# Gated linear attention with decays relative to the border of a chunk pair, one score product over 128 rows for both heads, and unscaled states

## The chip, the cores and the metric

The kernel runs on one core of a Trainium2 chip. Its engines work at the same time, each on its own list of instructions in order: TensorE (PE, with its weight loads as PEld), VectorE (DVE), ScalarE (ACT), GpSimd (POOL), and SP, which here issues most transfers. The metric is the device time of one execution in microseconds (us), as the median of several runs. TensorE's clock has two levels, 1.2 and 2.4 GHz; the profile gives the granted clock as a share of the higher one.

## What is computed

One layer of a hybrid trunk over 1024 tokens of width 1024, in float32: a normalised input is projected, three branches run on it (DeltaNet, gated linear attention, S5), are gated and summed, and a gated MLP and an embedding step follow. The change lies in the second branch, with 4 heads of key width 64 and value width 128:

```python
def gla_rule(q, k, v, g_log):
    q, k, v, g_log = map(to_chunks, (q, k, v, g_log))      # chunks of 64 tokens
    b = jnp.cumsum(g_log, axis=3)
    q_e = q * jnp.exp(b)
    k_e = k * jnp.exp(-b)
    attn = jnp.where(incl, jnp.einsum('bnhtd,bnhsd->bnhts', q_e, k_e), 0.0)
    intra = jnp.einsum('bnhts,bnhsv->bnhtv', attn, v)
    k_dec = k * jnp.exp(b[..., -1:, :] - b)
    dS = jnp.einsum('bnhck,bnhcv->bnhkv', k_dec, v)
    g_end = jnp.exp(b[..., -1, :])

    def step(S, inp):
        qe, ds, ge = inp
        o = jnp.einsum('bhck,bhkv->bhcv', qe, S)
        return ge[..., None] * S + ds, o
    ...
    o = intra + jnp.moveaxis(inter, 0, 1)
```

The head outputs are normalised, gated and go on to the merge of the branches.

## The kernel before

The work is laid out with features on the 128 partitions and the 1024 tokens along the free axis, two heads of gated linear attention to a tile (64 partitions each, a "pair"). Tokens go in 8 groups g of 128 (NG = 8), each a pair of chunks of 64.

Phase "1" runs the first norm, narrow (the small projections: rates of DeltaNet, and the log decays of gated linear attention, which are summed within a chunk and written to DRAM as gbd), and the four DeltaNet heads. Phase "2" runs the S5 blocks and gated linear attention in the order of the string ORDER, "P0 U0 U1 C0 A0 U2 C1 B0 U3 C2 A1 C3 B1": U and C are input and core of an S5 block, A is gla_prepare and B is gla_scan of a pair. Then come s5_glu, the output unit of S5, and the remaining gates. The later phases do the merge, the MLP and the output.

gla_prepare (line 702) loads the log decays, forms three exponentials (eb, ek, ed) and multiplies them by the row norm R, projects q and k (proj_in, 48 products of 128x512 each, in the split form hi/lo), and makes qe, q2, ke, kd and k2, where q2 and k2 carry an extra decay for the half of the group that lies across the border of its two chunks. k2 and the two heads' values are transposed on TensorE into kt and vt.

gla_scan (line 765) goes through the tokens in two halves of four groups. For each head and group, line 776 forms the scores from 64 partitions of ke and qe, and line 777 overwrites the quarter across the border from kd and qe. The scores are copied to SBUF (at) and masked, and line 791 multiplies them with the values; line 790 adds the part of the state, from 64 partitions of q2 and state. Line 796 forms the increment of the state (pd) and line 801 the new state. Then come head_norm of each head's outputs and, after both halves, gated_out with the projection of the gate.

In narrow, line 392 multiplies 64 partitions of nar with the constant both, and line 419 takes 48 partitions of the constant w2 and of nar.

Tiles of one tag share the slots of that tag (slot, with the counts given to phase); PSUM has two slots of [128, 1024] (big, tiles pb) and four of one bank (pst, tiles ps, pa, po, pd). A planner fixes the order of the instructions on each engine ahead of time by priorities; fill hands it gates (products of the branch gates, which need nothing from here) to be laid into gaps. In s5_glu, line 1045 loads the four S5 blocks into the slots qe, q2, ke and kd, and line 1054 puts two splits into vt.

Of the kernel before, what the change touches and what calls it, by code (L numbers as in the profile page):

```python
# [20 lines left out]
L = 1024  # L21
# [68 lines left out]
class Trunk:  # L90
# [212 lines left out]
    def constants(self):  # L303
# [36 lines left out]
        nc.gpsimd.memset(self.w2[64:128, :], 0.0)  # L340
        for p in (64, 96):
            self.dma("x", self.w2[p:p + 16, :], self.A["gla_w2"])
        self.both = c.tile([64, 8], F32, name="both")
        nc.gpsimd.tensor_copy(self.both, self.ident[0:64, 0:8])
# [40 lines left out]
    def narrow(self):  # L385
# [5 lines left out]
        for g in range(NG):  # L391
            self.mm(pt[:, g, :], self.nar[0:64, g * 128:(g + 1) * 128], self.both)
# [22 lines left out]
        for pair in range(2):  # L415
            x = self.slot(("kt", "vt")[pair])
            for t in (0, 512):
                pb = self.pst([128, 512])
                self.mm(pb, self.w2[64:112, pair * 128:(pair + 1) * 128], self.nar[64:112, t:t + 512])
                self.act(x[:, t:t + 512], pb, AF.Identity, bias=self.vec("gla_b2", pair, pair + 1))  # L420
# [281 lines left out]
    def gla_prepare(self, pair):  # L702
        nc = self.nc
# [3 lines left out]
        c64 = lambda ap: ap.rearrange("p (c t) -> p c t", t=64)  # L707
        bend = c64(gb)[:, :, 63:64].to_broadcast([128, 16, 64])
        eb, ek, ed = (self.slot(n) for n in ("qe", "ke", "kd"))
        self.sub(c64(ed), bend, c64(gb))  # L710
        self.act(ed, ed, AF.Exp, scale=1.0 / 16)
        self.act(eb, gb, AF.Exp, scale=1.0 / 16)
        self.act(ek, gb, AF.Exp, scale=-1.0 / 16)
        ee = self.sm([128, 16], "gla_ee")
        nc.vector.tensor_copy(ee, c64(eb)[:, :, 63])
        eev = ee.rearrange("p (g a) -> p g a", a=2)
        ge = self.sm([128, NG], "gla_ge")
        self.mul(ge, eev[:, :, 0], eev[:, :, 1])
        pair_v = lambda ap: ap.rearrange("p (g a t) -> p g a t", a=2, t=64)
        for e in (eb, ek, ed):  # L720
            self.mul(e, e, self.R)

        ps = self.proj_in(base)
        qe = eb
        self.stt(qe, ps, 0.125, eb, ALU.mult, ALU.mult)
        q2 = self.slot("q2")
        self.copy(pair_v(q2)[:, :, 0, :], pair_v(qe)[:, :, 0, :])
        self.mul(pair_v(q2)[:, :, 1, :], pair_v(qe)[:, :, 1, :],
                 eev[:, :, 0:1].to_broadcast([128, NG, 64]))
# [4 lines left out]
        kd = ed  # L734
        self.mul(kd, ps, ed)
        k2 = self.slot("t")
        self.copy(pair_v(k2)[:, :, 1, :], pair_v(kd)[:, :, 1, :])
        self.mul(pair_v(k2)[:, :, 0, :], pair_v(kd)[:, :, 0, :],
                 eev[:, :, 1:2].to_broadcast([128, NG, 64]))
        kt = self.slot("kt", (128, NG, 128))  # L740
        for half in range(2):
            pt = self.pst([128, 4, 128])
            for i in range(4):
                g = 4 * half + i
                self.tr(pt[:, i, :], k2[:, g * 128:(g + 1) * 128])
            self.copy(kt[:, 4 * half:4 * half + 4, :], pt)

        vt = []
        for hd in range(2):
# [3 lines left out]
            vtk = self.slot("vt", (128, NG, 128))  # L753
            for half in range(2):
# [4 lines left out]
                self.copy(vtk[:, 4 * half:4 * half + 4, :], pt)  # L759
            vt.append(vtk)  # L760
        self.fill("gla")
        return qe, q2, ke, kd, kt, vt, ge

    @ranked
    def gla_scan(self, pair, prepared):
        nc = self.nc
        qe, q2, ke, kd, kt, vt, ge = prepared
        state = None
        for half in range(2):
            ats, pos = [], []  # L770
            for hd in range(2):
                p0 = slice(64 * hd, 64 * hd + 64)
                pa = self.pst([128, 4, 128], "pa")
                for i in range(4):
                    t0 = (4 * half + i) * 128
                    self.mm(pa[:, i, :], ke[p0, t0:t0 + 128], qe[p0, t0:t0 + 128])
                    self.mm(pa[0:64, i, 64:128], kd[p0, t0:t0 + 64], qe[p0, t0 + 64:t0 + 128])
                at = self.t2k([128, 4, 128], "gla_at")
                self.copy(at, pa)
                nc.vector.copy_predicated(at, self.imask.unsqueeze(1).to_broadcast([128, 4, 128]),  # L780
                                          self.zero.unsqueeze(1).to_broadcast([128, 4, 128]))
                ats.append(at)
            for hd in range(2):
                pos.append(self.pst([128, 4, 128], "po"))
            for i in range(4):
                g = 4 * half + i
                for hd in range(2):
                    p0 = slice(64 * hd, 64 * hd + 64)
                    if state is not None:
                        self.mm(pos[hd][:, i, :], q2[p0, g * 128:(g + 1) * 128], state[p0, :], stop=False)  # L790
                    self.mm(pos[hd][:, i, :], ats[hd][:, i, :], vt[hd][:, g, :], start=state is None)
                if g < NG - 1:
                    pd = self.pst([128, 128], "pd")
                    for hd in range(2):
                        p0 = slice(64 * hd, 64 * hd + 64)
                        self.mm(pd[p0, :], kt[:, g, p0], vt[hd][:, g, :])
                    new = self.t5h([128, 128], "gstate")
                    if state is None:
                        nc.vector.tensor_copy(new, pd)
                    else:  # L800
                        self.stt(new, state, ge[:, g:g + 1], pd, ALU.mult, ALU.add)
                    state = new
            self.fill(f"gscan{half}")
            for hd in range(2):
                po = pos[hd]
# [784 lines left out]
```

## Time and profile before

| | us |
|---|---|
| median of 3 runs | 1924.6 (1923.9 to 1927.0) |
| profiled execution | 1922.1 |
| its span, first to last instruction | 1920.4 |
| TensorE busy | 1878.0 |
| VectorE busy | 1308.1 |
| ScalarE busy | 716.3 |
| first scan (gla_scan of pair 0) | 620.5 to 662.6 |
| second scan (pair 1) | 810.05 to 846.86 |

A busy time is the time in which at least one instruction of the engine runs. Matmuls overlap, so the distance between the starts of two of them tells what one costs, not its duration. In the rows further below "x8" is a count of instructions, a shape such as 64*128 behind a matmul is the part of TensorE's array that it uses (rows*columns), a float32 product is two instructions, and PEclk is the granted clock.

### The profile page before, as it was taken

How to read it: one execution, taken by the hardware profiler on the slowest of the kernel's cores; microseconds unless marked ns; L12 is line 12 of the kernel's file. 1: busy time of each engine (PE TensorE's matmuls, PEld its weight loads, DVE VectorE, ACT ScalarE, POOL GpSimd, SP SyncE). 2: the span in 40 equal slices, each digit the busy share in tenths (PEclk: the TensorE clock that was granted, in tenths of full speed). 3: DMA queues.
4: the chain of work that ended last, by engine and by line, in shares of the span. 5: the costliest groups of instructions: out<-in, count | busy, mean ns of one | idle time of the engine just before them, and what ended most of it. 6: DMA issues, size and time to landing. Idle time of an engine off the chain costs nothing.

```text
span 1920.4 us, 25126 instructions
## 1 busy us (share of the span) xinstructions
PE 1878.0 (98%) x9213; PEld 1535.8 (80%) x9213; DVE 1308.1 (68%) x2748; ACT 716.3 (37%) x1122; POOL 42.8 (2%) x64
## 2 busy tenths in 40 slices
PE   7999999999999999999899999999999999999998
PEld 5788887878888788777688878888888888878887
DVE  6898777765876576555467577787878774475446
ACT  5632332323423232323222444443434454363335
POOL 4000000000100000000000000000000000000000
PEclk9899999999999899989999999999999999999999
DMA  5123131221333133324754522222222257364332
GB/s 179 65 75 98 56 97 42 72 96 59 117 83 102 61 107 94 93 88 180 252 170 135 169 90 77 88 77 88 80 90 82 94 164 250 111 202 149 99 112 83
DMA packets 114844, 212.55 MB, mean 111 GB/s; under 512 B 25153, under 2 KB 38689, under 8 KB 114721
## 3 DMA queue, kind: packets, MB, share of 16 engines
q1 hardware_dynamic: 106080, 183.68, 29.9%
q10 hardware_dynamic: 8640, 27.27, 4.3%
q8 instruction: 72, 1.18, 0.2%
q14 instruction: 52, 0.42, 0.1%
HBM read 159.22 MB, written 51.68 MB: 110 GB/s over the span
## 4 chain that ended last, share of the span: by engine, by line
PE 71%; DVE 4%; ACT 1%; DMA 1%; issue 1%; POOLq 0%; DVEq 0%; ACTq 0%; POOL 0%
PE pb L166 35%; PE ps L166 31%; PE po L166 2%; PE pa L166 1%; DVE H L141 1%; PE ps L170 1%; DMA r<-yd 1%; PE pd L166 1%; DVE s_pa L141 0%; DVE s_pb L141 0%; PE pu L166 0%; DVE lo L141 0%; DMA raw<-cd 0%; DVE wl L141 0%; ACT hi L160 0%
## 5 line engine op out<-in xcount | busy, mean ns | idle before, releaser
L166 PE MATMUL pb<-hi,wh 128*128 128x512 f32 x1260 | 407.5, 400 | 17.1 <-DVE wh L141 8.1
L160 ACT ACTIVATE wh<-wr 128x512 fp32r<-128x512 f32 (+1 forms) x335 | 204.2, 614 | 573.0 <-PE pb L166 348.5
L166 PE MATMUL pb<-lo,wh 128*128 128x512 f32 x1260 | 403.9, 398 | 3.4 <-DVE lo L153 3.0
L166 PE MATMUL pb<-hi,wl 128*128 128x512 f32 x1244 | 399.3, 397 | 0.0
L141 DVE TENSOR_TENSOR wl<-wr,wh 128x512 fp32r<-128x512 f32 (+1 forms) x333 | 221.5, 669 | 196.9 <-ACT wh L160 187.6
L166 PEld LDWEIGHTS pb<-hi,wh 128*128 128x128 f32 x1260 | 236.7, 191 | 68.9 <-DVE wh L141 8.1
L166 PEld LDWEIGHTS pb<-lo,wh 128*128 128x128 f32 x1260 | 238.2, 190 | 55.3 <-DVE lo L153 4.7
L166 PEld LDWEIGHTS pb<-hi,wl 128*128 128x128 f32 x1244 | 234.1, 190 | 48.7 <-issue 2.6
L166 PE MATMUL ps<-hi,wh 128*128 128x512 f32 x442 | 172.8, 391 | 0.0
L166 PE MATMUL ps<-hi,wl 128*128 128x512 f32 x442 | 172.5, 390 | 0.0
L166 PE MATMUL ps<-lo,wh 128*128 128x512 f32 x442 | 172.4, 390 | 0.0
L166 PEld LDWEIGHTS ps<-hi,wh 128*128 128x128 f32 x442 | 83.3, 188 | 17.4
L166 PEld LDWEIGHTS ps<-hi,wl 128*128 128x128 f32 x442 | 83.2, 188 | 17.3
L166 PEld LDWEIGHTS ps<-lo,wh 128*128 128x128 f32 x442 | 83.2, 188 | 17.2
L160 ACT ACTIVATE fh<-wr 128x512 fp32r<-128x512 f32 x65 | 40.9, 632 | 114.7 <-PE ps L166 72.4
L153 DVE SCALAR_TENSOR_TENSOR c<-z,vecs,c 128x1023 f32<-128x1023 f32 (+1 forms) x44 | 56.5, 1284 | 6.9 <-ACT c L160 6.1
L166 PE MATMUL ps<-ph,wh 128*128 128x512 f32 (+1 forms) x128 | 49.2, 384 | 0.0
L166 PE MATMUL ps<-pl,wh 128*128 128x512 f32 (+1 forms) x128 | 48.5, 379 | 0.1
L166 PE MATMUL ps<-ph,wl 128*128 128x512 f32 (+1 forms) x128 | 48.3, 377 | 0.0
L141 DVE TENSOR_TENSOR z<-s,pb 128x512 f32<-128x512 f32 x44 | 30.2, 687 | 23.1 <-PE pb L166 23.1
L141 DVE TENSOR_TENSOR fl<-wr,fh 128x512 fp32r<-128x512 f32 x65 | 44.6, 688 | 1.8 <-ACT fh L160 1.8
L141 DVE TENSOR_TENSOR sgm<-pb,R 128x1024 f32<-128x1024 f32 x24 | 29.1, 1221 | 24.1 <-PE pb L166 24.0
(469 smaller groups left out, 3173.4 us busy)
## 6 DMA issues: line engine op xcount, KB each, us to landing
wr<-in_w_up SPq DMA_DIRECT2D x88, 256.0 KB, 2.8
wr<-in_w_down SPq DMA_DIRECT2D x80, 256.0 KB, 2.7
wr<-in_w_in SPq DMA_DIRECT2D x66, 256.0 KB, 3.2
wr<-in_w_gate SPq DMA_DIRECT2D x48, 256.0 KB, 2.9
gd<-sgm SPq DMA_DIRECT2D x24, 512.0 KB, 2.9
sgl<-gd ACTq DMA_DIRECT2D x24, 512.0 KB, 4.2
cd<-c SPq DMA_DIRECT2D x22, 512.0 KB, 2.6
wr<-in_w_ple_gate SPq DMA_DIRECT2D x32, 256.0 KB, 2.9
```

The costliest lines, as they stand in the source:

```text
L141: self.nc.vector.tensor_tensor(out=out, in0=a, in1=b, op=op)
L153: self.nc.vector.scalar_tensor_tensor(out=out, in0=a, scalar=s, in1=b, op0=op0, op1=op1)
L160: self.nc.scalar.activation(out, a, func, scale=scale, **kw)
L166: self.nc.tensor.matmul(out, lhsT=lhsT, rhs=rhs, start=start, stop=stop, **kw)
L170: self.nc.tensor.transpose(out, in_, self.ident[0:n, 0:n])
```

## The change

The log decays are taken relative to the border between the two chunks of a group: within the first chunk they are subtracted from the chunk's end, the second chunk counts from its start. With decays written so, one product over a whole group of 128 tokens gives the scores, and kd, q2 and k2 fall away. The queries of the two heads are written into one tile qm of [128, 2, 1024], for each head zero on the other head's 64 partitions, so that one product with all 128 partitions of ke gives the scores of both heads (256 columns). The states are kept unscaled (total); for the outputs a copy of the state, scaled by dec on ScalarE, is multiplied with all 128 partitions of qm. The increments of a half share one PSUM tile and come first. The values of both heads share one tile vt; s5_glu uses the slots qm, ke, kd and vt. In narrow the two small products take all 128 partitions, with zeros in the constants.

```diff
--- before.py
+++ after.py
@@ -337,11 +337,12 @@
         self.hbglu = c.tile([128, 4], F32, name="hbglu")
         nc.vector.tensor_scalar_mul(self.hbglu, self.vec("s5_b_glu"), 0.5)
         self.w2 = c.tile([128, 256], F32, name="w2")
-        nc.gpsimd.memset(self.w2[64:128, :], 0.0)
+        nc.gpsimd.memset(self.w2, 0.0)
         for p in (64, 96):
             self.dma("x", self.w2[p:p + 16, :], self.A["gla_w2"])
-        self.both = c.tile([64, 8], F32, name="both")
-        nc.gpsimd.tensor_copy(self.both, self.ident[0:64, 0:8])
+        self.both = c.tile([128, 8], F32, name="both")
+        nc.gpsimd.memset(self.both, 0.0)
+        nc.gpsimd.tensor_copy(self.both[0:32, :], self.ident[0:32, 0:8])
         nc.gpsimd.tensor_copy(self.both[32:64, :], self.ident[0:32, 0:8])
 
 
@@ -389,7 +390,7 @@
         self.mul(self.nar, ps, self.R)
         pt = self.pst([128, NG, 8])
         for g in range(NG):
-            self.mm(pt[:, g, :], self.nar[0:64, g * 128:(g + 1) * 128], self.both)
+            self.mm(pt[:, g, :], self.nar[:, g * 128:(g + 1) * 128], self.both)
         c = self.cpool
         sh = [128, HEADS, NG]
         b = self.sm(sh, "n_b")
@@ -416,7 +417,7 @@
             x = self.slot(("kt", "vt")[pair])
             for t in (0, 512):
                 pb = self.pst([128, 512])
-                self.mm(pb, self.w2[64:112, pair * 128:(pair + 1) * 128], self.nar[64:112, t:t + 512])
+                self.mm(pb, self.w2[:, pair * 128:(pair + 1) * 128], self.nar[:, t:t + 512])
                 self.act(x[:, t:t + 512], pb, AF.Identity, bias=self.vec("gla_b2", pair, pair + 1))
             ab = self.slot(("kt", "vt")[pair])
             self.stt(ab, x, -1.0, x, ALU.mult, ALU.max)
@@ -700,114 +701,116 @@
 
     @ranked
     def gla_prepare(self, pair):
+
         nc = self.nc
         base = 16 + 6 * pair
         gb = self.slot("t")
         self.dma("ld", gb, self.gbd[pair])
-        c64 = lambda ap: ap.rearrange("p (c t) -> p c t", t=64)
-        bend = c64(gb)[:, :, 63:64].to_broadcast([128, 16, 64])
-        eb, ek, ed = (self.slot(n) for n in ("qe", "ke", "kd"))
-        self.sub(c64(ed), bend, c64(gb))
-        self.act(ed, ed, AF.Exp, scale=1.0 / 16)
-        self.act(eb, gb, AF.Exp, scale=1.0 / 16)
-        self.act(ek, gb, AF.Exp, scale=-1.0 / 16)
-        ee = self.sm([128, 16], "gla_ee")
-        nc.vector.tensor_copy(ee, c64(eb)[:, :, 63])
-        eev = ee.rearrange("p (g a) -> p g a", a=2)
-        ge = self.sm([128, NG], "gla_ge")
-        self.mul(ge, eev[:, :, 0], eev[:, :, 1])
         pair_v = lambda ap: ap.rearrange("p (g a t) -> p g a t", a=2, t=64)
-        for e in (eb, ek, ed):
+        gv = pair_v(gb)
+        ee = self.sm([128, NG, 2], "gla_ee")
+        self.act(ee, gv[:, :, :, 63], AF.Exp, scale=1.0 / 16)
+        end = self.sm([128, NG, 1], "gla_end")
+        self.copy(end, gv[:, :, 0, 63:64])
+        self.sub(gv[:, :, 0, :], end.to_broadcast([128, NG, 64]), gv[:, :, 0, :])
+
+        dec = self.sm([128, NG - 1], "gla_dec")
+        self.mul(dec, ee[:, 0:NG - 1, 1], ee[:, 1:NG, 0])
+        eq, ek = self.slot("kd"), self.slot("ke")
+        for e, s in ((eq, 1.0 / 16), (ek, -1.0 / 16)):
+            self.act(pair_v(e)[:, :, 0, :], gv[:, :, 0, :], AF.Exp, scale=-s)
+            self.act(pair_v(e)[:, :, 1, :], gv[:, :, 1, :], AF.Exp, scale=s)
             self.mul(e, e, self.R)
 
+        qm = self.slot("qm", (128, 2, L))
+        for hd in range(2):
+            nc.gpsimd.memset(qm[64 - 64 * hd:128 - 64 * hd, hd, :], 0.0)
         ps = self.proj_in(base)
-        qe = eb
-        self.stt(qe, ps, 0.125, eb, ALU.mult, ALU.mult)
-        q2 = self.slot("q2")
-        self.copy(pair_v(q2)[:, :, 0, :], pair_v(qe)[:, :, 0, :])
-        self.mul(pair_v(q2)[:, :, 1, :], pair_v(qe)[:, :, 1, :],
-                 eev[:, :, 0:1].to_broadcast([128, NG, 64]))
+        for hd in range(2):
+            p0 = slice(64 * hd, 64 * hd + 64)
+            self.stt(qm[p0, hd, :], ps[p0, :], 0.125, eq[p0, :], ALU.mult, ALU.mult)
 
         ps = self.proj_in(base + 1)
         ke = ek
         self.mul(ke, ps, ek)
-        kd = ed
-        self.mul(kd, ps, ed)
-        k2 = self.slot("t")
-        self.copy(pair_v(k2)[:, :, 1, :], pair_v(kd)[:, :, 1, :])
-        self.mul(pair_v(k2)[:, :, 0, :], pair_v(kd)[:, :, 0, :],
-                 eev[:, :, 1:2].to_broadcast([128, NG, 64]))
         kt = self.slot("kt", (128, NG, 128))
         for half in range(2):
             pt = self.pst([128, 4, 128])
             for i in range(4):
                 g = 4 * half + i
-                self.tr(pt[:, i, :], k2[:, g * 128:(g + 1) * 128])
+                self.tr(pt[:, i, :], ke[:, g * 128:(g + 1) * 128])
             self.copy(kt[:, 4 * half:4 * half + 4, :], pt)
 
-        vt = []
+        vt = self.slot("vt", (128, NG, 2, 128))
         for hd in range(2):
             ps = self.proj_in(base + 2 + hd)
             vc = self.slot("t")
             self.mul(vc, ps, self.R)
-            vtk = self.slot("vt", (128, NG, 128))
             for half in range(2):
                 pt = self.pst([128, 4, 128])
                 for i in range(4):
                     g = 4 * half + i
                     self.tr(pt[:, i, :], vc[:, g * 128:(g + 1) * 128])
-                self.copy(vtk[:, 4 * half:4 * half + 4, :], pt)
-            vt.append(vtk)
+                self.copy(vt[:, 4 * half:4 * half + 4, hd, :], pt)
         self.fill("gla")
-        return qe, q2, ke, kd, kt, vt, ge
+        return qm, ke, kt, vt, dec
 
     @ranked
     def gla_scan(self, pair, prepared):
         nc = self.nc
-        qe, q2, ke, kd, kt, vt, ge = prepared
-        state = None
+        qm, ke, kt, vt, dec = prepared
+        sh = [128, 2, 2, 128]
+        flat = lambda t: t.rearrange("p i h t -> p (i h) t")
+        total = None
         for half in range(2):
-            ats, pos = [], []
-            for hd in range(2):
-                p0 = slice(64 * hd, 64 * hd + 64)
-                pa = self.pst([128, 4, 128], "pa")
-                for i in range(4):
-                    t0 = (4 * half + i) * 128
-                    self.mm(pa[:, i, :], ke[p0, t0:t0 + 128], qe[p0, t0:t0 + 128])
-                    self.mm(pa[0:64, i, 64:128], kd[p0, t0:t0 + 64], qe[p0, t0 + 64:t0 + 128])
-                at = self.t2k([128, 4, 128], "gla_at")
+            ats, pos, states = [], [], []
+            pd = self.pst([128, 4, 128], "pd")
+            for i in range(4):
+                g = 4 * half + i
+                if g < NG - 1:
+                    for hd in range(2):
+                        p0 = slice(64 * hd, 64 * hd + 64)
+                        self.mm(pd[p0, i, :], kt[:, g, p0], vt[:, g, hd, :])
+            for j in range(2):
+                pa = self.pst(sh, "pa")
+                for i in range(2):
+                    t0 = (4 * half + 2 * j + i) * 128
+                    self.mm(pa[:, i], ke[:, t0:t0 + 128], qm[:, :, t0:t0 + 128])
+                at = self.t2k(sh, "gla_at")
                 self.copy(at, pa)
-                nc.vector.copy_predicated(at, self.imask.unsqueeze(1).to_broadcast([128, 4, 128]),
+                nc.vector.copy_predicated(flat(at), self.imask.unsqueeze(1).to_broadcast([128, 4, 128]),
                                           self.zero.unsqueeze(1).to_broadcast([128, 4, 128]))
                 ats.append(at)
-            for hd in range(2):
-                pos.append(self.pst([128, 4, 128], "po"))
+            for i in range(4):
+                g = 4 * half + i
+                if g:
+                    states.append(self.tmp([128, 128], "gstate", "gstate", 4))
+                    self.copy(states[-1], total, scale=dec[:, g - 1:g])
+                if g < NG - 1:
+                    new = self.t5h([128, 128], "gtotal")
+                    if g == 0:
+                        nc.vector.tensor_copy(new, pd[:, i])
+                    else:
+                        self.stt(new, total, dec[:, g - 1:g], pd[:, i], ALU.mult, ALU.add)
+                    total = new
+            for j in range(2):
+                pos.append(self.pst(sh, "po"))
             for i in range(4):
                 g = 4 * half + i
                 for hd in range(2):
-                    p0 = slice(64 * hd, 64 * hd + 64)
-                    if state is not None:
-                        self.mm(pos[hd][:, i, :], q2[p0, g * 128:(g + 1) * 128], state[p0, :], stop=False)
-                    self.mm(pos[hd][:, i, :], ats[hd][:, i, :], vt[hd][:, g, :], start=state is None)
-                if g < NG - 1:
-                    pd = self.pst([128, 128], "pd")
-                    for hd in range(2):
-                        p0 = slice(64 * hd, 64 * hd + 64)
-                        self.mm(pd[p0, :], kt[:, g, p0], vt[hd][:, g, :])
-                    new = self.t5h([128, 128], "gstate")
-                    if state is None:
-                        nc.vector.tensor_copy(new, pd)
-                    else:
-                        self.stt(new, state, ge[:, g:g + 1], pd, ALU.mult, ALU.add)
-                    state = new
+                    po = pos[i // 2][:, i % 2, hd, :]
+                    if g:
+                        self.mm(po, qm[:, hd, g * 128:(g + 1) * 128], states[i - (half == 0)], stop=False)
+                    self.mm(po, ats[i // 2][:, i % 2, hd, :], vt[:, g, hd, :], start=g == 0)
             self.fill(f"gscan{half}")
-            for hd in range(2):
-                po = pos[hd]
+            for j in range(2):
+                po = flat(pos[j])
                 r = self.head_norm(po, 4)
-                self.mul(vt[hd][:, 4 * half:4 * half + 4, :], po, r.unsqueeze(2).to_broadcast([128, 4, 128]))
+                g0 = 4 * half + 2 * j
+                self.mul(flat(vt[:, g0:g0 + 2]), po, r.unsqueeze(2).to_broadcast([128, 4, 128]))
         for hd in range(2):
             hh = 2 * pair + hd
-            self.gated_out(self.proj_in(16 + 6 * pair + 4 + hd), vt[hd], self.hgla, "t", "t", self.yd[1][hh])
+            self.gated_out(self.proj_in(16 + 6 * pair + 4 + hd), vt[:, :, hd, :], self.hgla, "t", "t", self.yd[1][hh])
 
 
     def cmul(self, outr, outi, ar, ai, br, bi, tmp):
@@ -1040,18 +1043,19 @@
     @ranked
     def s5_glu(self):
         nc = self.nc
-        ys, raws = [], []
-        for q in range(4):
-            raw = self.slot(("qe", "q2", "ke", "kd")[q])
+        ys = []
+        qm = self.slot("qm", (128, 2, L))
+        raws = [qm[:, 0], qm[:, 1], self.slot("ke"), self.slot("kd")]
+        for q, raw in enumerate(raws):
             self.dma("ld", raw, self.y5d[q])
-            raws.append(raw)
             hi = self.slot(("up", "ub", "F", "H")[q], dt=F32R)
             lo = self.slot(("up", "ub", "M", "E")[q], dt=F32R)
             self.split(raw, hi, lo)
             ys.append((hi, lo))
         self.pt = []
+        his = self.slot("vt", (128, 2, L), F32R)
         for k in range(2):
-            hi, lo = self.slot("vt", dt=F32R), self.slot(("kt", "G")[k], dt=F32R)
+            hi, lo = his[:, k], self.slot(("kt", "G")[k], dt=F32R)
             raw = self.gpool.tile([128, L], F32, tag="sg", name="sgp", bufs=2)
             self.dma("ld", raw, self.A["pT"][k * 128:(k + 1) * 128, :])
             self.split(raw, hi, lo)
@@ -1480,8 +1484,8 @@
                         dn[h] = self.dn_prepare(h)
                     if h:
                         self.dn_scan(h - 1, dn.pop(h - 1))
-            slots = {t: 2 for t in ("up", "ub", "t", "vt")}
-            slots.update({t: 1 for t in ("F", "E", "G", "M", "H", "qe", "q2", "ke", "kd", "kt")})
+            slots = {t: 2 for t in ("up", "ub", "t")}
+            slots.update({t: 1 for t in ("F", "E", "G", "M", "H", "qm", "ke", "kd", "kt", "vt")})
             with self.phase("2", slots, {"t2k": 4, "t1k": 2, "t5h": 4}):
                 u, gl = {}, {}
                 U = lambda q: u.__setitem__(q, self.s5_in(q))
```

## Rows read from the trace of the kernel before

**Rows 1.** The page, part 1: busy us (share of the span) xinstructions.

```profile
PE 1878.0 (98%) x9213; PEld 1535.8 (80%) x9213; DVE 1308.1 (68%) x2748; ACT 716.3 (37%) x1122; POOL 42.8 (2%) x64
```

**Rows 2.** Windows, instructions on pb alone: window, length, PE busy (xcount), PEclk, DMA.

```profile
620.50:662.60 42.10, 13.19 (x34) 0.80 0.19 50
810.05:846.86 36.81, 9.60 (x22) 0.81 0.25 76
```

**Rows 3.** Windows in the scans: length, PE, PEld, DVE, ACT, POOL busy (xcount), PEclk, DMA.

```profile
624.00:630.50 6.50, 6.50 (x22) 4.90 (x22) 1.46 (x2) 0.60 (x1) 0.00 (x0) 0.50 0.27 44
...
641.00:651.70 10.70, 10.70 (x34) 7.90 (x35) 4.49 (x19) 1.12 (x2) 0.00 (x0) 0.53 0.40 138
```

**Rows 4.** Chain of waits: start us, us, what, ahead of the first scan.

```profile
496.67 20.90 PE pb L166 x92
...
617.07 3.57 PE ps L166 x32
```

**Rows 5.** Timeline of PE, scores: start us, us, engine, line, operation, array, shape, count.

```profile
621.24 0.49 PE L166 MATMUL pa<-qe,ke 64*128 64x128 f32 x2
621.65 0.33 PE L166 MATMUL pa<-qe,kd 64*64 64x64 f32 x2
621.90 0.49 PE L166 MATMUL pa<-qe,ke 64*128 64x128 f32 x2
...
625.06 0.79 PE L166 MATMUL pa<-qe,ke 64*128 64x128 f32 x2
625.78 0.47 PE L166 MATMUL pa<-qe,kd 64*64 64x64 f32 x2
```

**Rows 6.** Timeline of PE, increments and outputs of the first scan.

```profile
630.87 0.66 PE L166 MATMUL pd<-vt,kt 128*64 128x128 f32 x8
631.46 0.50 PE L166 MATMUL pb<-hi,wl 128*128 128x512 f32 x1
631.89 0.49 PE L166 MATMUL po<-gstate,q 64*128 64x128 f32 x2
632.30 0.49 PE L166 MATMUL po<-vt,gla_at 128*128 128x128 f32 x2
632.72 0.48 PE L166 MATMUL po<-gstate,q 64*128 64x128 f32 x2
```

**Rows 7.** Timeline of PE, the spread of the first norm.

```profile
46.22 1.03 PE L166 MATMUL ps<-rms_d,ones 128*128 128x256 f32 x4
46.89 0.58 PE L166 MATMUL ps<-hi,k 128*128 128x512 f32 x1
```

**Rows 8.** Windows ahead of the first scan.

```profile
486.00:620.50 134.50, 134.50 (x718) 112.97 (x716) 106.94 (x388) 50.05 (x95) 13.08 (x22) 1.00 0.34 106
```

**Rows 9.** One window of the same kind and the timeline of PE, narrow.

```profile
54.00:64.00 10.00, 10.00 (x17) 4.60 (x16) 7.15 (x9) 6.15 (x8) 0.00 (x0) 0.50 0.00 0
...
57.44 3.78 PE L166 MATMUL ps<-w,w 48*128 48x512 f32 x4
```

**Rows 10.** Tiles qe and ud: operation, xcount: ns min/median/max, first and last start, shape.

```profile
L141 DVE TENSOR_TENSOR qe<-qe,R x2: 1211/1215/1219, 517.6 to 692.3; 128x1024 f32<-128x1024 f32 x2
...
L160 ACT ACTIVATE ud<-pu,cd x28: 348/367/369, 206.6 to 484.0; 128x128 f32<-128x128 f32 x28
```

**Rows 11.** Timeline of SP, its queue in the second scan.

```profile
833.67 0.34 SPq L113 DMA_DIRECT2D qe<-y5d  x1
...
834.71 0.32 SPq L113 DMA_DIRECT2D M<-s5y  x1
...
858.46 0.33 SPq L113 DMA_DIRECT2D kd<-y5d  x1
```

**Rows 12.** Timeline of DVE behind the second scan.

```profile
848.79 1.28 DVE L153 SCALAR_TENSOR_TENSOR M<-up,vecs,M 128x1024 f32<-128x1024 f32 x1
...
863.75 1.22 DVE L141 TENSOR_TENSOR E<-kd,H 128x1024 fp32r<-128x1024 f32 x1
```

**Rows 13.** Timeline of PE, start of s5_glu.

```profile
866.75 1.20 PE L166 MATMUL pb<-up,wh 128*128 128x512 f32 x4 [0.47 <-DVE t L141]
```

## The prediction

> **What bounds the kernel now.** I read the page's busy times first: TensorE is busy for 1878.0 of 1920.4 us, VectorE for 68% [rows 1]. So the question about any edit is how much TensorE time it takes away, and whether what feeds TensorE keeps pace afterwards. Next I read the stages by windows. The two scans of gated linear attention (gla_scan, one for each pair of heads) run at 620.5 to 662.6 us and at 810.05 to 846.86 us [rows 2]. TensorE is busy all the time there, but not at its full clock: in the two long slow stretches of the first scan the granted clock is 0.50 and 0.53, so nearly throughout at the lower level, 1.2 GHz [rows 3], and over either scan it is 0.80 [rows 2]. Then I read TensorE in order of time and along the chain of waits, because a busy time can't tell a fast matmul from a slow one: the distance from one start to the next can.
>
> At the full clock an instruction of a projection (128x512) takes 20.90 / 92 = 0.227 us, and one of the full-shape float32 products of the S5 stage, just ahead of the first scan, 3.57 / 32 = 0.112 us; such a product is two instructions, 0.223 us [rows 4]. The score products of the scan are dearer although they are smaller: at the full clock a call with 64 rows takes 0.41 us and the 64x64 call behind it 0.25 us, at the low level the former takes 0.72 us [rows 5]. The output products show that it isn't the 64 rows alone: a 64-row call (state) and a 128-row call (values) alternate there, and either takes 0.41 us [rows 6]. A full call beside calls of another tile shape costs nearly twice what it costs among its like.
>
> **What the change takes away in the scans.** First the scans as they are. In the first window 34 instructions of projections and gates (tile pb) lie between the scan's own, in the second 22 [rows 2]; at 0.227 us these are 7.7 and 5.0 us, and four transposes in the first are 0.4 us. The scans proper thus cost 42.1 - 8.1 = 34.0 us and 36.8 - 5.0 = 31.8 us, together 65.8 us, low clock included.
>
> After the change, for each pair of heads:
> - Scores: eight calls of 128 rows and 256 columns in place of 32 calls of half the rows. The nearest row is the spread of the norm, four 256-column float32 instructions in 0.67 us, 0.17 us each [rows 7]; twice the 128-column instruction is 0.22 us. I take the dearer, since it holds over a longer stretch: 16 x 0.22 = 3.5 us.
> - Outputs: 16 calls with the values and 14 with the states, all 128x128 now: 30 x 0.223 = 6.7 us. If they kept today's 0.41 us: 12.3 us.
> - State increments (pd): 28 instructions of 64 columns as before, now in two blocks. Eight took 0.59 us [rows 6], so 2.1 us; four changes of shape at 0.19 us (0.41 less 0.22) are 0.8 us.
>
> That is 13.1 us for a pair, 26.2 us for both, so 65.8 - 26.2 = 39.6 us less, if the clock stays full. I expect that: the S5 products, full calls too, run at 1.00 to the end of their stretch [rows 8], and the clock fell only after some microseconds of the half-row calls (the rows at 621 us are still at full price, those at 625 us are not [rows 5]).
>
> Here a rule speaks against the change. The rows say that a 64-row call costs 0.41 us, more than a full one. The Trainium skill, TensorEngine Tiling (Array Packing), section Performance Considerations, recommends two-fold row tiling for a contraction of at most 64, two calls side by side in the array; padding with zeros gives that up. By the rule the old half-row calls would cost half of a full one, the scans some 10 us a pair, and the change would add about 5 us in all. The trace disagrees: one head's calls follow one another on the same rows, shapes alternate, and nothing runs side by side. What the old calls cost is measured, so the rule gets no chance here.
>
> **The small products of narrow.** They take 64 and 48 rows now and 128 afterwards. From 54 to 64 us the granted clock is 0.50 with TensorE busy throughout; four 48-row instructions take 3.8 us [rows 9]. At the full clock these 10 us of work are 5.0 us. So between 0 (the clock falls anyway) and 5.0 us; VectorE, busy for 7.15 of the 10 us [rows 9], follows, so I count 3.5 us.
>
> **What moves on the other engines.** For each pair gla_prepare loses on VectorE the product kd, a multiplication by R (1.215 us each [rows 10]), two half-size products and half a subtraction, and gains a second 64-partition product of 1.215 us: some 3 us less. ScalarE has less to do as well. POOL gets two memsets. All this lies beside projections: in 486 to 620.5 us TensorE is busy for 134.50 of 134.50 us [rows 8]. I cost it at nothing; without that cover a memset that waits for its tile could cost 2 us. That the two value tiles of a pair become one slot costs nothing either: the second pair's scan comes 147 us after the first's [rows 2], so the slot is long free. The larger memsets of w2 and both lie in the first microseconds, and narrow reads them after 50 us. In the scan ScalarE gets 14 scaled copies of the state; the like in DeltaNet takes 0.367 us [rows 10]. They stand between a state and its output products, 5.1 us in all, but the next state doesn't wait for them, and increments, scores and projections can run meanwhile: between 0 and 5.1 us, I take 0, as today's scans leave TensorE no idle time [rows 2].
>
> **Where it can be given back.** Behind the second scan stands the S5 output unit (s5_glu), which needs the last S5 block by way of DRAM. Its load M<-s5y is issued on SP's queue at 834.71 us, behind the load of qe, which had waited until the scan had read its last scores (833.67) [rows 11]. From 848.79 us VectorE works on it, and its last split starts at 863.75 and takes 1.22 us: 16.2 us [rows 12]. TensorE begins the unit at 866.75 us [rows 13], so today the projections behind the scan (from 846.86 us) cover the chain with 1.8 us to spare. In the new kernel the first two loads go into qm, which is read until the last output product. If M<-s5y stays behind them, it is issued only at the scan's end; an estimate of 3 us for it to land (for kd's load it is under 5.3 us, from its issue at 858.46 [rows 11] to the split at 863.75) makes the chain 19.2 us from there against 19.9 us of cover, and two splits that can be done ahead today come on top. So 0 to 10 us; I take 2 us, nearer to the low end, as the chain's own work is unchanged.
>
> **Sum against the profiled run.** 39.6 + 3.5 - 2 = 41.1 us. The profiled execution took 1922.1 us (span 1920.4), 2.5 us under the median of the runs, 1924.6. On the median's scale 1924.6 - 41.1 = 1883.5 us; since shorter scans leave VectorE's chains less cover in places that I can't name, I allow 1.5 us more: 1885 us.
>
> **Rivals.**
> 1. The clock falls all the same, so the change does only half of what it can. The scans' 26.2 us and the 12.7 us of projections among them then run for perhaps half of the time at about 1.7 times their price (0.72 against 0.41): some 13 us lost, and narrow's 3.5 us: 1901 us. For it: no row of before shows a stretch of the new kind, with half of qm zeros and increments of half the columns. Against it: the S5 stretch [rows 8]. Chance 0.12.
> 2. The tail takes it back: behind the second scan the chain is uncovered by 10 to 20 us, 1894 to 1904 us. For it: only 1.8 us to spare, and VectorE works in a fixed order. Against it: its work is the same, and M<-s5y may be placed ahead of the loads into qm. Chance 0.16.
> 3. Slower: the increments of a half now share one PSUM tile that is held until the last of them is added, beside two tiles of scores and two of outputs, five for four slots. The second half's tiles then wait until the first half's norm has read its outputs; if VectorE has long work queued ahead of that norm, TensorE stands still. It turns slower from 10.3 us of uncovered waiting in each of the four halves (41.1 / 4); with 14 us each, 1940 us. Against it: today's second halves wait for the same norm, and projections fill that time [rows 2]. Chance 0.04.
>
> **How the numbers follow.** Forecast 0.65 (its own range 1877 to 1894), clock 0.12, tail 0.16, slower 0.04, little change for reasons not named 0.03. The range takes in the forecast, the clock and most of the tail: 1877 to 1902. Its low end is both gains whole (39.6 + 5.0 us) with the cheaper price of the scores (1.6 us), 1878 us, and 1 us for the spread of the runs. About 0.2% is what a measurement of this kernel can tell from no change: faster by more 0.93, within it 0.03, slower 0.04.
>
> **What would show it.** Right: in the trace of after output calls stand 0.22 us apart, the granted clock is 1.00 in both scans and from 54 to 64 us, and the scans cost about 13 us each without what lies between. Wrong: the low clock in the scans (rival 1); TensorE idle behind the second scan, ended by VectorE's splits (rival 2); TensorE idle ahead of a second half's scores or outputs (rival 3).

## The result

| | before | after |
|---|---|---|
| median, us (four runs; three of after) | 1924.5 | 1893.1 |
| ratio, with its 95% interval | | 0.9830 (0.9809 to 0.9852) |
| profiled execution, us | 1922.1 | 1889.1 |
| its span, us | 1920.4 | 1887.3 |

A fourth run of after took 3076.4 us at a granted clock of 0.56 and is left out here; the other three took 1889.1 to 1894.7 us, and with it the median is 1893.9 us. So the change brings 31.4 us by the medians (the profiled executions stand 33.0 us apart). Forecast was 1885 us: the time lies in the range, 8.1 us above its likeliest value.

### The profile of after

The page of after, its busy times [rows 1 for before] and its granted clock in 40 slices (9 is 0.9 or more); the last line is the clock of before:

```profile
PE 1844.1 (98%) x9117; PEld 1510.4 (80%) x9117; DVE 1303.5 (69%) x2740; ACT 718.7 (38%) x1138; POOL 49.6 (3%) x69
...
PEclk9999999999999999999999999999999999999999
```

```profile
PEclk9899999999999899989999999999999999999999
```

TensorE is busy 33.9 us less, and no slice of after falls below 0.9, where three of before do. The windows of the two scans (window, length, PE busy and count, granted clock, DMA) answer to [rows 2]:

```profile
617.17:632.20 15.03, 15.03 (x118) 1.00 0.25 66
786.14:800.20 14.06, 14.06 (x113) 1.00 0.28 86
```

The scans take 15.0 and 14.1 us in place of 42.1 and 36.8, though with 11 and 8 projection instructions between their own instead of 34 and 22. The timeline of TensorE in the first scan answers to [rows 5, 6]:

```profile
617.17 1.09 PE L166 MATMUL pd<-vt,kt 128*64 128x128 f32 x16
618.19 1.99 PE L166 MATMUL pa<-qm,ke 128*128 128x256 f32 x8
619.84 0.81 PE L166 MATMUL pb<-hi,wl 128*128 128x512 f32 x2
...
621.40 0.39 PE L166 MATMUL po<-gstate,qm 128*128 128x128 f32 x2
621.62 0.39 PE L166 MATMUL po<-vt,gla_at 128*128 128x128 f32 x2
621.85 0.39 PE L166 MATMUL po<-gstate,qm 128*128 128x128 f32 x2
```

An output call follows the one before it by 0.22 us, where it was 0.41; a score instruction takes (619.84 - 618.19) / 8 = 0.206 us, an increment 1.02 / 16 = 0.064 us.

So far the forecast holds. What it lacks comes later. S5's output unit starts at 824.54 us, 42.2 us ahead of [rows 13]:

```profile
824.54 1.09 PE L166 MATMUL pb<-up,wh 128*128 128x512 f32 x4
```

The tile Xh then shows when its products begin and end in the MLP's up stage: the view gives count, duration of one in ns (min/median/max), first and last start. First of before, then of after:

```profile
L166 PE MATMUL ps<-Xh,wh x90: 388/390/632, 1140.8 to 1563.7; 128*128 128x512 f32 x90
```

```profile
L166 PE MATMUL ps<-Xh,wh x90: 392/397/496, 1099.2 to 1531.0; 128*128 128x512 f32 x90
```

After is 41.6 us ahead at the first of them and 32.7 us at the last: 8.9 us are lost in a stage in which the change has not touched a line. A window in the middle of it, of before and of after:

```profile
1200.00:1400.00 200.00, 200.00 (x884) 1.00 0.25 85
```

```profile
1200.00:1400.00 200.00, 200.00 (x864) 1.00 0.25 84
```

TensorE is busy all the time and at its full clock in both, and gets through 20 instructions fewer: 0.2315 us each in place of 0.2262.

### The profile page after: what moved, and what is told of

It is laid out like the page before. It is cut to its first block, busy times and chain, and to the rows that moved or that the text cites. A ratio compares the mean times of both kernels' runs of the same rounds, so it can differ in the third digit from the quotient of the medians.

```text
span 1887.3 us, 24948 instructions
## 1 busy us (share of the span) xinstructions
PE 1844.1 (98%) x9117; PEld 1510.4 (80%) x9117; DVE 1303.5 (69%) x2740; ACT 718.7 (38%) x1138; POOL 49.6 (3%) x69
## 4 chain that ended last, share of the span: by engine, by line
PE 71%; DVE 3%; DMA 1%; ACT 1%; issue 1%; POOLq 0%; DVEq 0%; ACTq 0%; POOL 0%
PE pb L166 37%; PE ps L166 31%; PE po L166 1%; PE ps L170 1%; DMA raw<-cd 1%; DMA r<-yd 1%; DVE H L141 0%; PE pd L166 0%; PE pa L166 0%; DVE lo L141 0%; PE pu L166 0%; ACT hi L160 0%; DVE s_pa L141 0%; DVE s_pb L141 0%; DVE wl L141 0%
```

## Experiments: the loss in the MLP

What the two kernels differ in there is where the tiles lie in SBUF. The change adds two kinds of small tiles, gla_end and gla_dec, and drops gla_ge; each is held in two slots of 32 bytes per partition, so the pool of small tiles grew by 64 bytes. All that the compiler puts behind it, Xh, Xl, the split MLP weights fh, fl and the tiles of every phase among it, moved by 64 bytes: Xh's pool from byte 113856 of each partition to 113920. What lies ahead stayed: hi and lo from 9408, wr, wh and wl from 74944. Theory A is the place; theory B is that this execution happened to be slow.

**The changed kernel again**, as the yardstick (no edit).

> The changed kernel once more, as the yardstick for the three others on the same chip. Theory A (the matmuls of the first MLP products run 2% slower because every tile behind the small tiles has moved by 64 bytes per partition in SBUF) and theory B (that execution happened to be slow there) both expect a median near 1892 us against 1924. They differ in the window from 1200 to 1400 us: A expects 864 matmuls there again (0.2315 us from start to start), B 880 or more.

Measured: 1888.9 us, ratio 0.9819 (0.9804 to 0.9833), 865 instructions in the window. The loss is there again, so it is not the chance of one execution.

**The old addresses.**

```diff
-        end = self.sm([128, NG, 1], "gla_end")
+        end = self.sm([128, NG, 1], "gla_end", bufs=1)
...
-        dec = self.sm([128, NG - 1], "gla_dec")
+        dec = self.sm([128, NG - 1], "gla_dec", bufs=1)
```

> The changed kernel with one slot in place of two for the small tiles gla_end and gla_dec, so that the small tiles take 64 bytes per partition less and all later tiles lie at the addresses of the kernel before; the order of the instructions stays as it is. Theory A (place): 882 to 885 matmuls from 1200 to 1400 us, and about 9 us less than the changed kernel, 1880 to 1886 us. Theory B (not the place): 864 as in the changed kernel, and the same time within 2 us.

Measured: 1876.4 us, ratio 0.9754 (0.9740 to 0.9769), 12.5 us less than the changed kernel, more than the 9 us expected. Window and tile:

```profile
1200.00:1400.00 200.00, 200.00 (x884) 1.00 0.25 82
```

```profile
L166 PE MATMUL ps<-Xh,wh x90: 389/389/499, 1100.0 to 1521.4; 128*128 128x512 f32 x90
```

The stage starts when it did in after (1100.0 against 1099.2 us) and ends 9.6 us sooner. Against e3_after, whose profiled execution took 11.0 us longer, the stage gives 10.4 us of that (421.4 us in place of 431.8 from the first of these products to the last). The duration of a product is 389 ns nearly throughout, where it scatters from 392 to 397 and beyond in after. This version beats both kernels.

**The kernel before, moved by 64 bytes.**

```diff
+        self.sm([128, NG], "gla_x")
```

> The kernel before with one small tile more that nothing uses, so that all later tiles move by the same 64 bytes per partition as in the changed kernel. Theory A (place): about 864 matmuls from 1200 to 1400 us in place of 884, and about 9 us more than before, 1931 to 1935 us. Theory B: the same as before within 2 us.

Measured: 1934.1 us, ratio 1.0053 (1.0037 to 1.0070): a tile that nothing reads makes the old kernel 10.5 us slower. In the profiled execution 7.4 us are lost in this stage (430.3 us in place of 422.9), and its window is that of after:

```profile
1200.00:1400.00 200.00, 200.00 (x864) 1.00 0.25 84
```

Theory A stands, in both directions. What about the place is it that counts? Four more runs change unused tiles: in three of them only the size of the one ahead of the small tiles (PAD) in the changed kernel; the fourth, e9_all_shift64, takes the version with the old addresses and adds a new one ahead of everything.

```diff
-PAD = 32
+PAD = 96
```

> The changed kernel with an unused tile 64 bytes larger, so that all tiles behind it lie 128 bytes further than in the kernel before (64 further than in the changed kernel). If the price of a matmul hangs on the place in steps of 128 bytes: 882 to 885 matmuls from 1200 to 1400 us, and 1876 to 1879 us. If the best place is a single address, or if more bytes are worse: 864 or fewer, and 1888 us or more.

```diff
         self.mpool.tile([128, PAD // 4], F32, name="pad", bufs=1)
+        self.cpool.tile([128, 16], F32, name="pad_all")
```

> The version with the old addresses, and an unused tile of 64 bytes ahead of everything, so that the split weights (wh, wl) move by the same 64 bytes as Xh, Xl and the rest, which then lie at the same addresses as in the changed kernel. If it is the relation of the two operands' addresses that counts: 882 to 885 matmuls from 1200 to 1400 us, and 1876 to 1879 us. If it is the address of Xh and Xl by itself: 864, and 1888 us or more.

PAD = 224 and PAD = 480:

> The changed kernel with an unused tile that is larger, so that Xh, Xl and all tiles behind the small ones lie 256 bytes further than in the kernel before, while the weights stay; in the kernel before the two lie 38912 bytes apart, 19 x 2048. Since 64 and 128 bytes more were both slow: if the distance counts in steps of 256, 884 matmuls from 1200 to 1400 us and 1876 to 1879 us; in steps of 512 or more, 865 to 870 and 1888 us or more.

> The same with 512 bytes more than in the kernel before. If the distance counts in steps of 256 or 512: 884 matmuls from 1200 to 1400 us and 1876 to 1879 us. In steps of 1024 or more: 865 to 870 and 1888 us or more.

Measured, all together (moved: bytes per partition against the kernel before; instructions from 1200 to 1400 us):

| kernel | Xh, Xl, fh, fl moved | hi, lo, wr, wh, wl moved | instructions | median, us | ratio to before |
|---|---|---|---|---|---|
| before | 0 | 0 | 884 | 1922.4 to 1924.1 | 1 |
| e2_before_shift64 | 64 | 0 | 864 | 1934.1 | 1.0053 |
| e3_after | 64 | 0 | 865 | 1888.9 | 0.9819 |
| e8_after_shift128 | 128 | 0 | 869 | 1890.1 | 0.9835 |
| e10_shift256 | 256 | 0 | 885 | 1877.1 | 0.9756 |
| e10_shift512 | 512 | 0 | 884 | 1878.1 | 0.9760 |
| e1_after_old_addr | 0 | 0 | 884 | 1876.4 | 0.9754 |
| e9_all_shift64 | 64 | 64 | 884 | 1878.3 | 0.9772 |

So it is not the address of Xh or fh by itself: in e9_all_shift64 both lie where they lie in after, and the price is the good one. It is how far they have moved against what lies ahead of the small tiles, and of the moves tried, 0, 256 and 512 bytes are good, 64 and 128 are not. My expectation named the two operands of one product as the pair whose distance counts, and that is too narrow. The product of Xh and fh has both operands among the moved tiles, at the same addresses in after and in e9_all_shift64, and yet its duration differs; the tile view of after, then of e9_all_shift64:

```profile
L166 PE MATMUL pb<-Xh,fh x88: 388/392/397, 1112.0 to 1533.8; 128*128 128x512 f32 x88
```

```profile
L167 PE MATMUL pb<-Xh,fh x88: 389/389/389, 1109.5 to 1522.4; 128*128 128x512 f32 x88
```

Whether it is slowed by the products ahead of it in the stream, or by other engines that read wr at the same time, no run here tells. The mechanism stays open; the size is measured, and so are the distances at which it appears. The Trainium skill, SBUF — State Buffer, section Who interferes with whom, lets accesses hold one another up on the port pair that VectorE and GpSimd share and nowhere else; by that rule no distance between tiles could make a matmul wait for another access. Whether such waits are behind the 864 instructions against 884, no run here tells.

## Experiments: the scans

**Narrow alone**: the kernel before with the full-row constants, which get their zeros as in the change.

```diff
...
-            self.mm(pt[:, g, :], self.nar[0:64, g * 128:(g + 1) * 128], self.both)
+            self.mm(pt[:, g, :], self.nar[:, g * 128:(g + 1) * 128], self.both)
...
-                self.mm(pb, self.w2[64:112, pair * 128:(pair + 1) * 128], self.nar[64:112, t:t + 512])
+                self.mm(pb, self.w2[:, pair * 128:(pair + 1) * 128], self.nar[:, t:t + 512])
```

> The kernel before with the narrow part of the change alone (the two small products on all 128 partitions). If rows of 128 keep the clock up: granted clock 1.00 from 54 to 64 us, the first scan 3 to 4 us earlier with its low clock as before, and 3 to 5 us less in all, 1920 to 1922 us. If the clock there falls for another reason: 0.5 as before and no gain.

Measured: 1918.4 us, ratio 0.9971 (0.9960 to 0.9982), 5.2 us less. Windows of this kernel in narrow [rows 9] and in the scores of its first scan:

```profile
54.00:57.00 3.00, 3.00 (x10) 1.00 0.00 0
57.00:60.00 3.00, 3.00 (x12) 1.00 0.00 0
...
622.00:627.00 5.00, 5.00 (x19) 0.50 0.34 59
```

The clock is full in narrow, and falls in the scan as before: what narrow does is not what lowers it in the scan. In before the clock stands at 0.50 from 54 us [rows 9], behind these products of 64 and 48 rows:

```profile
51.43 1.39 PE L166 MATMUL ps<-both,w 64*128 64x8 f32 x11
...
53.10 2.40 PE L166 MATMUL ps<-w,w 48*128 48x512 f32 x3
```

Both kinds were widened together, so which of them lowers it there this run does not tell.

**Scores from 64 rows again, all of one shape.**

```diff
-                    self.mm(pa[:, i], ke[:, t0:t0 + 128], qm[:, :, t0:t0 + 128])
+                    self.mm(pa[:, i], ke[p0, t0:t0 + 128], qm[p0, hd, t0:t0 + 128])
```

(within a loop over heads in place of pairs of groups; the mask and the outputs follow)

> The changed kernel with its scores formed for each head from 64 partitions again (16 calls of 64 rows and 128 columns for each pair in place of 8 of 128 rows and 256 columns), all of one shape in a row. If 64 rows alone cost 0.41 us a call: 0.41 us from start to start, 16 x 0.41 - 3.5 = 3.1 us more for each pair, and if the clock falls in them too, 6 us or more in all, 1895 us or later. If only a change of shape costs: 0.22 us a call, the same price as the calls they replace, and within 2 us of the changed kernel.

Timeline of TensorE, first scan:

```profile
620.00 1.71 PE L166 MATMUL pa<-qm,ke 64*128 64x128 f32 x16
621.64 0.73 PE L166 MATMUL pb<-hi,wl 128*128 128x512 f32 x2
```

Sixteen instructions in 621.64 - 620.00 = 1.64 us, 0.103 each: a 64-row call costs 0.21 us, and two of them, one for each head, cost what the padded call of both heads costs, 2 x 0.206 us. The granted clock is 1.00 in every window of 5 us of the first scan. So 64 rows among their like are neither dear here nor do they lower the clock. The median is 1891.8 us, 2.9 above the yardstick, where I expected at most 2; the score calls explain none of that. Of the 2.4 us between the profiled executions, 0.6 lie ahead of the first scan, 1.0 between the starts of the two scans and 0.8 from there to S5's output unit; in the first scan four output instructions take 0.83 us from 623.17 us, where four took 0.44 in e3_after. Why they come later was not followed.

**State products from 64 rows, in turn with those of 128.**

```diff
-                        self.mm(po, qm[:, hd, g * 128:(g + 1) * 128], states[i - (half == 0)], stop=False)
+                        self.mm(po, qm[p0, hd, g * 128:(g + 1) * 128], states[i - (half == 0)][p0, :], stop=False)
```

(the tiles of the outputs are again one for each head, not one for each pair of groups)

> The changed kernel with the products of the states taken from 64 partitions, so that calls of 64 and of 128 rows alternate in the outputs as they did before. If the alternation costs 0.19 us at each change: 0.41 us from start to start, 5.6 us more for each pair, 11 us in all (1900 us), and with the clock at its lower level there up to 20 us. If the old price came from something else (the quarter products, the state's own chain): 0.22 us and the time of the changed kernel, 1889 us.

Timeline and window of TensorE, first scan:

```profile
624.12 0.48 PE L166 MATMUL po<-gstate,qm 64*128 64x128 f32 x2
624.54 0.49 PE L166 MATMUL po<-vt,gla_at 128*128 128x128 f32 x2
624.96 0.49 PE L166 MATMUL po<-gstate,qm 64*128 64x128 f32 x2
```

```profile
622.00:627.00 5.00, 5.00 (x26) 1.00 0.49 122
```

A call every 0.42 us, as before the change: the change of shape is what costs, 0.19 us each time. The median is 1899.0 us, ratio 0.9881 against 0.9819, so 10 to 12 us, as the 0.19 us give. But the clock stays at 1.00 in both scans. Taking turns between 64 and 128 rows does not lower it over these stretches of 5 us.

**The old scan without its quarter products**, which then are the remaining suspect.

```diff
-                    self.mm(pa[0:64, i, 64:128], kd[p0, t0:t0 + 64], qe[p0, t0 + 64:t0 + 128])
```

> The kernel before without the 64x64 products across the chunk border (this part of the scores is left out), so that its score calls are all of one shape, 64 rows and 128 columns, in a row; the outputs alternate as before. If the changes of shape make the price and the quarter products lower the clock: 0.21 us a score call, the clock at 1.00 in the scores and perhaps in the outputs too, and up to 32 x 0.45 = 14 us less for each pair at the full clock, 25 to 35 us less in all with the clock, 1889 to 1899 us. If the half-row calls lower it by themselves: 0.41 us a call, the clock falls to 0.50 in the scores as before, and about 8 us less for each pair for the calls left out, some 1908 us.

Measured: 1895.9 us, ratio 0.9855 (0.9841 to 0.9870). That is 28.2 us less, as expected, but not by the sum that I gave: at the full clock a pair saves 16 x 0.66 - 16 x 0.21 = 7.2 us, not 14; the rest I put down to the clock. The sixteen score instructions of a half take 1.71 us here too, and the clock is 1.00 where it was 0.50 [rows 3]:

```profile
622.00:627.00 5.00, 4.98 (x37) 1.00 0.59 92
...
642.00:647.00 5.00, 5.00 (x29) 1.00 0.01 2
```

The outputs alternate at 0.42 us as before. That leaves two readings: the quarter products themselves, or that they took turns with the others.

**The quarter products behind the others**: nothing left out, only the order within a score tile.

```diff
                     self.mm(pa[:, i, :], ke[p0, t0:t0 + 128], qe[p0, t0:t0 + 128])
+                for i in range(4):
+                    t0 = (4 * half + i) * 128
                     self.mm(pa[0:64, i, 64:128], kd[p0, t0:t0 + 64], qe[p0, t0 + 64:t0 + 128])
```

> The kernel before with the four 64x64 products of a score tile behind its four 64-row products, in place of in turn with them; nothing is left out. It tells what the run without the quarter products leaves open: whether these products or the changes of shape between them and the others lower the clock. If the changes do (64 for each pair before, 8 here): the clock at 1.00 in both scans, 0.21 us for a 64-row call, some 9 to 11 us less for each pair and 4 to 7 us more from the clock, 1894 to 1902 us. If the quarter products themselves do: the clock falls to 0.50 behind the scores again, some 1906 us or later.

Measured: 1901.3 us, ratio 0.9891 (0.9867 to 0.9915): 22.4 us less than before from the order of 64 products (a pair has 32 changes between the two shapes in before, not the 64 that I wrote). Timeline and window of TensorE:

```profile
620.64 1.16 PE L166 MATMUL pa<-qe,ke 64*128 64x128 f32 x8
621.73 0.68 PE L166 MATMUL pa<-qe,kd 64*64 64x64 f32 x8
622.33 1.16 PE L166 MATMUL pa<-qe,ke 64*128 64x128 f32 x8
```

```profile
622.00:627.00 5.00, 5.00 (x42) 1.00 0.67 105
```

Four 64-row calls and four quarter calls take 622.33 - 620.64 = 1.69 us; in turn they took 4 x 0.66 = 2.64 us at the full clock [rows 5], and more once it had fallen. The clock is 1.00 in both scans. It was the taking of turns that did both; whether the clock answers to the turns themselves or to the longer time that they take, these runs do not separate.

## Why the prediction was right, and where not

- **Scores, outputs, increments.** 13.1 us a pair were forecast. The scans less what lies between: 15.0 - 11 x 0.227 - 0.4 (two transposes and the end of the S5 products) = 12.1 us, and 14.1 - 8 x 0.227 - 0.1 = 12.2 us, so 65.8 - 24.3 = 41.5 us less in place of 39.6, 1.9 us more. The 0.22 us for outputs held; the score instruction was 0.206, not 0.22, and 28 increments took 1.8 us, not 2.1. That changes of shape cost 0.19 us is shown by e6_state_64rows, not only read from [rows 5, 6].
- **The clock.** It stays full in both scans and in narrow, as forecast: rival 1 did not happen. After, in narrow (length, PE, PEld, DVE, ACT, POOL busy, PEclk, DMA):

```profile
54.00:57.00 3.00, 3.00 (x10) 1.68 (x9) 3.00 (x6) 2.80 (x5) 0.00 (x0) 1.00 0.00 0
57.00:60.00 3.00, 3.00 (x14) 2.44 (x14) 3.00 (x4) 2.97 (x4) 0.00 (x0) 1.00 0.00 0
```

  The reason that I gave for the scans, that the half-row calls lower it, was too wide: 64-row calls in a row keep it there, and 64 and 128 rows in turn keep it over stretches of 5 us. In the scans only the 64-row and quarter products in turn lowered it. In narrow it fell behind 64-row products of 8 columns and 48-row products, and full rows keep it up (e4_narrow_only).
- **Narrow.** 3.5 us forecast; the first scan starts 3.4 us sooner (620.57 to 617.17), 3.2 if counted from the spread of the first norm [rows 7], which begins at 46.22 and 46.05 us, and alone it brings 5.2 us, by its interval 3.5 to 7.7.
- **The tail.** The load of M is issued right behind the two loads into qm, as the forecast had it:

```profile
800.27 0.82 SPq L113 DMA_DIRECT2D qm<-y5d  x2
801.32 0.32 SPq L113 DMA_DIRECT2D M<-s5y  x1
```

  But nothing was given back: from the scan's end to the start of the unit TensorE is busy for 23.9 of 24.3 us.

```profile
800.20:824.50 24.30, 23.86 (x114) 1.00 0.54 194
```

  I had 0 to 10 us and took 2; it is 0.4. VectorE works on M from 808.56 us, 7.2 us behind the issue of its load. There are 24.3 us of cover in place of 19.9, since more projections are left behind the scan (114 instructions in place of 94). Rival 2 did not happen. But my picture of the chain was wrong, and the low price is partly luck: from that issue to the end of the last split it takes 25.7 us, where I had 19.2 and two splits on top, and the last split starts 1.3 us behind the first product of the unit:

```profile
825.83 1.22 DVE L141 TENSOR_TENSOR E<-kd,H 128x1024 fp32r<-128x1024 f32 x1 [0.88 <-ACT H L160]
```

  It costs nothing, because the unit's products that read E come only from 829.1 us: the unit doesn't wait for the last split, as I had read from [rows 12, 13].
- **Five tiles for four slots** (rival 3): TensorE has no idle time in either scan.
- **The sum.** 41.1 us were forecast, and at the start of the S5 unit 42.2 us are there. The step that failed is one that the sum does not have: it took it for granted that stages without an edit keep their price. The MLP's up stage took 8.9 us back, because of 64 bytes in a pool of small tiles. That the time still lies in the forecast's own range (1877 to 1894) is luck: that range held no such loss. The prediction gave 0.03 to little change for reasons not named; the diff did show the two new tiles, but nothing in the trace of before says that a place has a price.
- **Without that loss** the change is worth 44.1 to 47.2 us (the medians of the four kernels with the good price, each against before), 3 to 6 us more than the sum. The traces show 1.9 us of that in the scans and 1.6 in the tail; the rest was not followed. The 1.5 us that I allowed on top for chains that lose cover was not needed.
- **Zeros in place of packing.** The Trainium skill, TensorEngine Tiling (Array Packing), section Performance Considerations, recommends two-fold row tiling where the contraction has at most 64 rows. e5_scores_64rows shows what 64-row calls cost one after another: two of them, one for each head, as much as the padded call of both. What two of them side by side would cost, no run here shows.

## What to carry to other kernels

Look at the distance between starts of small products and at the order of their shapes: grouping products of one shape brought about half of what rewriting them did (22 us against 41 here, by moving one line into a loop of its own). After any change that adds or drops a tile, compare the count of instructions in a window of a stage that was not touched; if it fell at the same clock, give the tile pool its old size back, or pad it until what lies behind it has moved by 256 bytes (here 256 and 512 were as good as none).

## What was not expected of the hardware

- A matmul's price hangs on where tiles lie in SBUF. 64 or 128 bytes more per partition between the tiles ahead of the small ones and those behind them cost 1.7 to 2.3% of TensorE's rate in the MLP's up stage (884 to 869 or 864 instructions in 200 us) at a granted clock of 1.00; 0, 256 and 512 bytes cost nothing, nor did 64 bytes for all tiles together.
- A change between calls of 64 and of 128 rows costs 0.19 us, and 64-row calls among their like cost nothing extra (0.21 us a call).
- The granted clock fell to 0.50 with TensorE busy throughout, where 64-row and 64x64 products took turns, and stayed at 1.00 when the same products were sorted by shape. In narrow too it fell with TensorE busy, behind products of 64 and 48 rows, and stayed at 1.00 with 128 rows in their place.
